# Twelve linear units of a state-space stage as fp32 matmuls on unsplit operands

## The chip, the cores and the metric

The kernel runs on one core of a Trainium2 chip. A core has five engines with a queue each: TensorE (PE in the profile; its weight loads are listed apart as PEld), VectorE (DVE), ScalarE (ACT), GpSimd (POOL) and SyncE (SP, which here only issues DMAs). Each queue runs in order; semaphores connect them. The metric is the time of one execution on the device in microseconds; smaller is better.

## The reference

A two-layer streaming encoder of 256 tokens and 2048 channels: a state-space mixer (S5), a gated convolutional feed-forward, then latent attention and a second feed-forward, all in fp32. The change lies in the mixer's last step, a gated linear unit on the mixer's output:

```python
y = ys.transpose(1, 0, 2, 3, 4).reshape(Bsz, S, D_MODEL)   # 256 x 2048
y = jax.nn.gelu(y)
val, gate = jnp.split(y @ w_glu + b_glu, 2, axis=-1)       # w_glu: 2048 x 4096
return val * jax.nn.sigmoid(gate)
```

## The kernel before

**How an fp32 product is made.** Weights and activations are split into two float32r parts, hi (an ACT copy, line 73) and lo (a DVE subtraction, line 74). `mm3` (lines 108 to 110) then adds three float32r products, hi by hi, hi by lo and lo by hi. `wunit` (line 79 issues the load) brings one weight unit of 512 x 512 (1 MB, tile `raw`, two buffers) and splits it in two halves into `whi` and `wlo`, three buffers each. A unit is used for both token blocks `tb` of 128 tokens: 2 x 4 x 3 = 24 matmuls of 512 columns into two `acc` banks of PSUM.

**The state-space stage** (`s5`). Its loop has 18 iterations over 16 sub-blocks, software-pipelined: iteration n runs part_k and part_e of sub-block n, part_v, part_r and part_h of n-1 and part_c of n-2. After every fourth sub-block part_d turns a quarter of the mixer's output around (PE transposes, line 550) and splits it into `act{q}`: for two halves hh and two token blocks, four ACT copies and four DVE subtractions of 128 x 256. A quarter q of the 2048 input channels then allows four units of the gated linear unit (`glu_steps`, n and half), and the loop runs one such unit per iteration. So units 1 to 4 (quarter 0), 5 to 8 (quarter 1) and 9 to 12 (quarter 2) lie in the stage, the last ones at its end; units 13 to 16 (quarter 3) and the sixteen of `glu_rest` come behind it. `glu_early` adds each unit's banks to the accumulator `f`: an ACT copy for quarter 0 (line 256), a DVE addition for the others (line 258).

**Names in PE's order.** Within an iteration the rows are V (part_v, `ET`, line 399), C and H (part_c, `TP` and `H`, line 399), vs (part_r's transposes of `vs`, lines 497 and 498), U (line 442), k (part_k, `f` and `e`, line 399), E (part_e, line 481), K (part_k's 32 small matmuls, line 467) and R (part_h, line 513). On DVE w1 and w2 are lines 500 and 501, K is 452, f1 and f2 are 430 and 431, e1 and e2 433 to 435.

**What sets the order.** A tile scheduler orders the instructions of each engine when the program is built; tiles of a pool are reused in a ring, so a load into `raw` waits until the last reader of the tile two loads earlier is done.

Of the kernel before, what the change touches and what calls it, by code (L numbers as in the profile page):

```python
# [8 lines left out]
F32 = mybir.dt.float32  # L9
F32R = mybir.dt.float32r  # L10
I32 = mybir.dt.int32
AF = mybir.ActivationFunctionType
# [3 lines left out]
P = 128  # L16
D = 2048
S = 256
NB = S // P
# [25 lines left out]
def tile_trunk(ctx: ExitStack, tc: tile.TileContext, a: dict):  # L45
    nc = tc.nc
    act, dve, pool, pe, sync = nc.scalar, nc.vector, nc.gpsimd, nc.tensor, nc.sync
    cnt = [0]

    def T(pl, shape, dt=F32, tag=None, bufs=None):  # L50
        cnt[0] += 1
        kw = {"bufs": bufs} if bufs else {}
        return pl.tile(shape, dt, tag=tag, name=f"{tag}_{cnt[0]}", **kw)
# [3 lines left out]
    env = {"wp": ctx.enter_context(tc.tile_pool(name="wp", bufs=2)), "wb": 3}  # L57
# [4 lines left out]
    def wk():  # L62
        return T(ps, [P, 512], F32, "wk")

    def accb():
        return T(ps, [P, 512], F32, "acc")
# [5 lines left out]
    def split(hi, lo, src, eng=None):  # L72
        act.activation(hi, src, AF.Copy)  # L73
        (eng or dve).tensor_tensor(lo, src, hi.bitcast(F32), op=ALU.subtract)  # L74
# [32 lines left out]
    def mm3(o, lh, ll, rh, rl, first, last):  # L107
        pe.matmul(o, lh, rh, start=first, stop=False)  # L108
        pe.matmul(o, lh, rl, start=False, stop=False)  # L109
        pe.matmul(o, ll, rh, start=False, stop=last)  # L110
# [88 lines left out]
    def act_tiles():  # L199
        A.append(T(aa, [P, 4, 2, S], F32R, f"act{len(A)}"))  # L200

    def acts4(tb, q, ks):
        ts_ = slice(tb * P, (tb + 1) * P)
        return A[q][:, ks, 0, ts_], A[q][:, ks, 1, ts_]

    def acts(tb, kt):
        return acts4(tb, kt // 4, kt % 4)
# [22 lines left out]
    glu_w = a["w_glu"].rearrange("(j b p) n -> b p j n", j=4, p=P)  # L230

    def glu_load(n, b, half, slots=(None, None)):
        col = half * D + n * 512
        return wunit(glu_w[b][:, :, col : col + 512], 4, 512, slots=slots)

    def glu_mm(bank, b, tb, halves):
        hk, u = halves
        for i, (wh, wl) in enumerate(u):
            for k in range(hk):
                j = i * hk + k  # L240
                mm3(bank, *acts(tb, 4 * b + j), wh[:, k, :], wl[:, k, :], b == 0 and j == 0, b == 3 and j == 3)

    def glu_early(f, n, b, half):
        hv = glu_load(n, b, half)
        banks = [accb(), accb()]
        for tb in range(NB):
            hk, u = hv
            for i, (wh, wl) in enumerate(u):
                for k in range(hk):
                    j = i * hk + k  # L250
                    mm3(banks[tb], *acts(tb, 4 * b + j), wh[:, k, :], wl[:, k, :], j == 0, j == 3)
        o = half * 1024 + n * 512
        for tb in range(NB):
            c = f[tb][:, o : o + 512]
            if b == 0:
                act.activation(c, banks[tb], AF.Copy)
            else:
                dve.tensor_tensor(c, banks[tb], c, op=ALU.add)


    def s5(f):
        with tc.tile_pool(name="s5", bufs=2) as q1:
# [128 lines left out]
            PB = 32 // NP  # L391
# [84 lines left out]
            def part_e(e1):  # L476
                ET = T(q1, [P, NP, P], F32, "ET", 1)
                for w in range(NG):
                    ptv = wk().rearrange("p (g t) -> p g t", g=4)
                    for g in range(4):  # L480
                        pe.transpose(ptv[:, g, :], e1[:, 4 * w + g].rearrange("p s q -> p (s q)"), ident)
                    act.activation(ET[:, 4 * w : 4 * w + 4, :], ptv, AF.Copy)
                return ET

            def part_v(U, ET):
                pvg = by_group(tiled((lambda g, j: U[:, g, 32 * j : 32 * j + 32], lambda g, j: ET[:, 4 * g + j, :])))
                vs = T(q1, [P, NG, 192], F32, "vs", 1)
                act.activation(vs[:, :, 0:P], pvg, AF.Copy)
                act.activation(vs[:, :, P:192], pvg[:, :, 0:64], AF.Copy)
                return vs  # L490

            def part_r(sb, vs, si, co):
                pvv = wk()
                pvt, pvs = pvv[:, :W], pvv[:, W : 2 * W]
                for g in range(NG):
                    o = slice(g * P, (g + 1) * P)
                    pe.transpose(pvt[:, o], vs[:, g, 0:P], ident)
                    pe.transpose(pvs[:, o], vs[:, g, 64:192], ident)
                w1, w2 = T(q1, [P, W], F32, "w1"), T(q1, [P, W], F32, "w2")
                dve.tensor_tensor(w1, pvt, co, op=ALU.mult)  # L500
                dve.tensor_tensor(w2, pvs, si, op=ALU.mult)
                dve.tensor_tensor(w1, w1, w2, op=ALU.add)
                dc = Ds[sb % 2]
                act.activation(
                    dc[:, :, 1:32], mag8[:, NP * sb : NP * sb + NP].unsqueeze(2).to_broadcast([P, NP, 31]), AF.Copy
                )
                R = T(q1, [P, W], F32, "R")
                dve.tensor_tensor_scan(R, dc.rearrange("p n c -> p (n c)"), w1, 0.0, op0=ALU.mult, op1=ALU.add)
                return R
# [15 lines left out]
            def part_c(sb, yg, ff, U, TP, H):  # L525
                def h(g, j):
                    return H[:, 4 * g + j, :]

                py = tiled(
                    (lambda g, j: U[:, g, 32 * j : 32 * j + 32], lambda g, j: TP[:, j, g * P : (g + 1) * P]),  # L530
                    *((h, lambda g, j, z=z: flat2(z[:, 4 * g + j, 0:8, :])) for z in ff),
                )
                o = (sb % PB) * 16 * NG
                act.activation(
                    yg[:, :, o : o + 16 * NG].rearrange("p t (g q) -> p g t q", q=16),
                    py.rearrange("p (g t q) -> p g t q", g=NG, q=16),
                    AF.Gelu_apprx_tanh,
                )

            def glu_steps(b):  # L540
                for n in range(2):
                    for half in range(2):
                        yield glu_early(f, n, b, half)

            def part_d(qt, yg):
                act_tiles()
                for hh in range(2):
                    ptv = wk().rearrange("p (t m) -> p t m", t=4)
                    for t in range(4):
                        pe.transpose(ptv[:, t, :], yg[:, 7 - (4 * hh + t), :], ident)  # L550

                    def av(z):
                        return z.rearrange("p j (c t) -> p t j c", t=8)[:, 4 * hh : 4 * hh + 4]

                    for tb in range(NB):
                        hi, lo = acts4(tb, qt, slice(0, 4))
                        split(av(hi), av(lo), ptv.rearrange("p t (j c) -> p t j c", j=4)[:, :, :, 16 * tb : 16 * tb + 16])

            todo, ab, fr, U, TP, ET, H = [], {}, {}, {}, {}, {}, {}
            nb = 4 * PB  # L560

            def lead(n):
                if n >= nb:
                    return
                if n % PB == 0:
                    z[0] = powers(n // PB)
                ab[n] = part_a(n, z[0])
                if n % FR == 0:
                    si, co = frames(n // FR)
                    for k in range(FR):  # L570
                        fr[n + k] = (si[k], co[k])
# [5 lines left out]
            for n in range(nb + 2):  # L577
                if 0 <= n - 1 < nb:
                    vs = part_v(U[n - 1], ET.pop(n - 1))
                if n >= 2:  # L580
                    m = n - 2
                    if m % PB == 0:
                        yg = T(q1, [P, 8, P], F32, "yg", 1)
                    part_c(m, yg, ab.pop(m)[1], U.pop(m), TP.pop(m), H.pop(m))
                if 0 <= n - 1 < nb:
                    R = part_r(n - 1, vs, *fr[n - 1])
                if n < nb:
                    U[n], TP[n] = part_k(n, *ab[n])
                    ET[n] = part_e(ab[n][0])
                if 0 <= n - 1 < nb:  # L590
                    H[n - 1] = part_h(n - 1, R, *fr.pop(n - 1))
                if n >= 2 and m % PB == PB - 1:
                    part_d(m // PB, yg)
                    todo.append(glu_steps(m // PB))
                lead(n + 1)
                if n < 3:
                    scale_x(rs, n + 1)
                if todo and next(todo[0], True) is True:
                    todo.pop(0)
# [454 lines left out]
    f = f_pair()  # L1054
    todo = s5(f)
# [21 lines left out]
    with tc.tile_pool(name="gl", bufs=2) as q1:  # L1077
        gs, f, fst, done = begin(ng[0, 1], ng[0, 2], f=f)
# [100 lines left out]
```

## Time and profile before

| | us |
|---|---|
| median of 3 runs (lowest, highest) | 2193.63 (2193.27, 2194.26) |
| the profiled execution | 2187.58 |
| its span, first to last instruction | 2185.8 |
| state-space stage with its exit, in the span | about 20 to 313 |

The span is the time from the first to the last instruction on the core; the profile's times count from its start. Most of the span is the two feed-forwards and the attention, which the change does not touch. In the timeline a row is a start, a duration, an engine, a line, the tile written and those read, a count, and in brackets how long the engine had been idle and what ended that. Back-to-back matmuls overlap: their distance is that of their starts, not their duration.

### The profile page before, as it was taken

What the parts mean: (1) busy time and instruction counts of PE and PEld (TensorE: products, weight loads), DVE (VectorE), ACT (ScalarE), POOL (GpSimd) and SP (SyncE); (2) the same over time, 40 slices, a digit from 0 to 9 for tenths busy, and PEclk for the clock granted to TensorE, in tenths of its full rate; (3) what the DMA queues carried; (4) which work ended last, traced back from release to release, by engine and by line L of the source; (5) the groups of instructions that cost most, each with busy time, mean ns of one, the idle gap of its engine ahead of it and who ended that gap; (6) DMA issues with size and microseconds to landing.
All of it is one profiled execution on the core that took longest, in us unless ns stands there. A gap on an engine that the chain in (4) does not pass through costs nothing.

```text
span 2185.8 us, 32404 instructions
## 1 busy us (share of the span) xinstructions
PE 2079.0 (95%) x13268; PEld 1764.2 (81%) x13268; DVE 1408.8 (64%) x1940; ACT 1122.4 (51%) x1695; POOL 19.8 (1%) x57
## 2 busy tenths in 40 slices
PE   3788999899999999999989999989999999999998
PEld 2566777888888888888878998788888888888886
DVE  7999666666466556655686665566646655665567
ACT  6677445455455445544464554545545544554444
POOL 0000000000000000000000000000000000000000
PEclk9999999999999999999999999999999999999999
DMA  4132476455565555555564434635555555555654
GB/s 131 50 98 75 154 233 206 145 188 179 193 197 187 193 193 191 178 190 193 192 200 129 136 118 155 212 123 189 189 193 193 180 187 193 193 183 184 194 191 154
DMA packets 280966, 374.74 MB, mean 171 GB/s; under 512 B 9200, under 2 KB 196208, under 8 KB 279792
## 3 DMA queue, kind: packets, MB, share of 16 engines
q1 hardware_dynamic: 280816, 372.66, 52.4%
q8 instruction: 104, 1.70, 0.3%
q14 instruction: 46, 0.38, 0.1%
HBM read 370.54 MB, written 2.10 MB: 170 GB/s over the span
## 4 chain that ended last, share of the span: by engine, by line
PE 82%; DVE 10%; DMA 4%; ACT 3%; issue 1%; POOL 0%; SPq 0%; DVEq 0%; POOLq 0%; ACTq 0%
PE wk L114 29%; PE wk L115 15%; PE acc L108 9%; PE acc L109 9%; PE acc L110 9%; DMA raw<-in_w_glu 3%; PE wk L108 2%; PE wk L109 2%; PE wk L110 2%; DVE wlo L74 2%; PE acc L191 1%; DVE x L74 1%; ACT whi L73 1%; DVE f L431 1%; DVE f L430 1%
## 5 line engine op out<-in xcount | busy, mean ns | idle before, releaser
L74 DVE TENSOR_TENSOR wlo<-raw,whi 128x1024 fp32r<-128x1024 f32 (+2 forms) x640 | 761.0, 1191 | 584.0 <-ACT whi L73 579.3
L73 ACT ACTIVATE whi<-raw 128x1024 fp32r<-128x1024 f32 (+2 forms) x640 | 658.3, 1031 | 635.3 <-PE wk L114 245.6
L114 PE MATMUL wk<-act,whi 128*128 128x512 f32 x2688 | 941.9, 395 | 0.0
L115 PE MATMUL wk<-act,wlo 128*128 128x256 f32 x2688 | 753.0, 280 | 0.0
L114 PEld LDWEIGHTS wk<-act,whi 128*128 128x128 f32 x2688 | 504.1, 188 | 119.3
L115 PEld LDWEIGHTS wk<-act,wlo 128*128 128x128 f32 x2688 | 507.4, 189 | 0.3
L108 PE MATMUL acc<-whi,hh 128*128 128x512 f32 x652 | 255.4, 392 | 0.0
L109 PE MATMUL acc<-wlo,hh 128*128 128x512 f32 x652 | 255.3, 392 | 0.0
L110 PE MATMUL acc<-whi,hl 128*128 128x512 f32 x652 | 254.3, 391 | 0.0
L108 PEld LDWEIGHTS acc<-whi,hh 128*128 128x128 f32 x652 | 122.4, 188 | 27.2 <-ACT hh L73 0.5
L109 PEld LDWEIGHTS acc<-wlo,hh 128*128 128x128 f32 x652 | 122.4, 188 | 27.0 <-DVE wlo L74 0.5
L110 PEld LDWEIGHTS acc<-whi,hl 128*128 128x128 f32 x652 | 122.4, 188 | 26.9
L108 PE MATMUL acc<-whi,act 128*128 128x512 f32 (+1 forms) x332 | 126.4, 381 | 2.7 <-ACT act L73 2.7
L109 PE MATMUL acc<-wlo,act 128*128 128x512 f32 (+1 forms) x332 | 124.9, 377 | 1.9 <-DVE wlo L74 1.9
L110 PE MATMUL acc<-whi,act 128*128 128x512 f32 (+1 forms) x332 | 124.3, 375 | 0.1
L765 DVE SCALAR_TENSOR_TENSOR cv<-gs,cw,cv 128x255 f32<-128x255 f32 (+1 forms) x168 | 77.2, 480 | 3.0
L109 PEld LDWEIGHTS acc<-wlo,act 128*128 128x128 f32 x332 | 62.5, 188 | 14.9 <-DVE wlo L74 4.0
L108 PEld LDWEIGHTS acc<-whi,act 128*128 128x128 f32 x332 | 62.5, 188 | 14.5 <-ACT act L73 3.0
L110 PEld LDWEIGHTS acc<-whi,act 128*128 128x128 f32 x332 | 62.5, 188 | 11.5 <-DVE act L74 0.5
L763 ACT ACTIVATE cv<-gs,cb,cw 128x256 f32<-128x256 f32 x84 | 50.5, 601 | 36.5 <-DVE gs L715 36.5
L714 ACT ACTIVATE us<-wk 128x256 f32<-128x256 f32 x84 | 31.7, 380 | 60.3 <-PE wk L115 60.3
L714 ACT ACTIVATE gs<-wk 128x256 f32<-128x256 f32 x84 | 32.0, 381 | 59.8 <-PE wk L115 59.8
(282 smaller groups left out, 2342.5 us busy)
## 6 DMA issues: line engine op xcount, KB each, us to landing
raw<-in_w_gate SPq DMA_DIRECT2D x88, 1024.0 KB, 5.0
raw<-in_w_up SPq DMA_DIRECT2D x88, 1024.0 KB, 4.9
raw<-in_w_down SPq DMA_DIRECT2D x88, 1024.0 KB, 4.9
raw<-in_w_glu SPq DMA_DIRECT2D x32, 1024.0 KB, 6.2
raw<-in_w_o SPq DMA_DIRECT2D x16, 1024.0 KB, 4.9
raw<-in_w_ukv SPq DMA_DIRECT2D x8, 1024.0 KB, 5.3
gb<-in_norm_g SPq DMA_DIRECT2D x6, 1024.0 KB, 6.7
raw<-in_w_uq SPq DMA_DIRECT2D x8, 768.0 KB, 4.4
```

The source lines that it names most:

```text
L73: act.activation(hi, src, AF.Copy)
L74: (eng or dve).tensor_tensor(lo, src, hi.bitcast(F32), op=ALU.subtract)
L108: pe.matmul(o, lh, rh, start=first, stop=False)
L109: pe.matmul(o, lh, rl, start=False, stop=False)
L110: pe.matmul(o, ll, rh, start=False, stop=last)
L114: pe.matmul(ov, lh, r, start=first, stop=False)
L115: pe.matmul(ov[:, 0, :], ll, r[:, 0, :], start=False, stop=last)
L191: pe.matmul(ptv[:, k, :], h[:, o : o + P], d, start=True, stop=True)
L430: dve.tensor_tensor(f1, zt(0, 0, 9, 1), bc(2, 9), op=ALU.mult)
L714: act.activation(z[:, ft, :], two[ft][:, S:], AF.Copy)
L763: act.activation(cv[:, ft, :], gv[:, ft, :], AF.Identity, scale=cw[:, 2, n : n + 1], bias=cb[:, n : n + 1])
L765: dve.scalar_tensor_tensor(cv[:, ft, sh:], gv[:, ft, : S - sh], cw[:, 2 - sh, n : n + 1], cv[:, ft, sh:], op0=ALU.mult, op1=ALU.add,)
```

## The change

The twelve units of quarters 0 to 2 no longer split their weights. `glu_full` loads `raw` and hands it to PE as fp32, together with `ax`, an unsplit fp32 copy of the quarter's activations that part_d now writes beside `act{q}` (one buffer). A unit is 2 x 4 = 8 fp32 matmuls of 512 columns. The split activations are still made, since `glu_rest` uses them. Units 13 and later are as before. The accumulation into `f` is moved into `glu_keep`, unchanged.

```diff
+    def glu_full(f, n, b, half, ax):
+        raw = T(env["wp"], [P, 4, 512], F32, "raw")
+        col = half * D + n * 512
+        sync.dma_start(raw, glu_w[b][:, :, col : col + 512])
+        banks = [accb(), accb()]
+        for tb in range(NB):
+            for j in range(4):
+                pe.matmul(banks[tb], ax[:, j, tb * P : (tb + 1) * P], raw[:, j, :], start=j == 0, stop=j == 3)
+        glu_keep(f, n, b, half, banks)
...
+        glu_keep(f, n, b, half, banks)
+
+    def glu_keep(f, n, b, half, banks):
         o = half * 1024 + n * 512
...
-            def glu_steps(b):
+            def glu_steps(b, ax):
                 for n in range(2):
                     for half in range(2):
-                        yield glu_early(f, n, b, half)
+                        yield glu_early(f, n, b, half) if ax is None else glu_full(f, n, b, half, ax)
...
+                ax = None if qt == 3 else T(q1, [P, 4, S], F32, "ax", 1)
...
-                        split(av(hi), av(lo), ptv.rearrange("p t (j c) -> p t j c", j=4)[:, :, :, 16 * tb : 16 * tb + 16])
+                        src = ptv.rearrange("p t (j c) -> p t j c", j=4)[:, :, :, 16 * tb : 16 * tb + 16]
+                        if ax is not None:
+                            act.activation(av(ax[:, :, tb * P : (tb + 1) * P]), src, AF.Copy)
+                        split(av(hi), av(lo), src)
+                return ax
...
-                    part_d(m // PB, yg)
-                    todo.append(glu_steps(m // PB))
+                    todo.append(glu_steps(m // PB, part_d(m // PB, yg)))
```

The scheduler's order moves at three places. Line numbers grow by 13 to 17 behind the new functions: line 399 becomes 412, 473 becomes 486, 488 and 489 become 501 and 502. The first place is PE's queue around unit 1, behind quarter 0's transposes, before:

```order
L550 MATMUL wk_1131<-cst_73,yg_514 128x128 x4
L399 MATMUL wk_1203<-ET_1101,U_1043 32x128 x8
L399 MATMUL wk_1216<-TP_915,U_894 32x128 x4
L399 MATMUL wk_1216<-f_168_823,H_47_184 32x128 x4
L399 MATMUL wk_1216<-f_169_824,H_47_184 32x128 x4
L399 MATMUL wk_1216<-TP_915,U_894 32x128 x4
L399 MATMUL wk_1216<-f_168_823,H_47_184 32x128 x4
L399 MATMUL wk_1216<-f_169_824,H_47_184 32x128 x4
L108 MATMUL acc_1175<-whi_1167,act_218_1121 128x512
```

and now:

```order
L412 MATMUL wk_1184<-ET_1101,U_1043 32x128 x8
L412 MATMUL wk_1197<-TP_915,U_894 32x128 x4
L250 MATMUL acc_1172<-raw_1170,ax_1122 128x512 x4
L250 MATMUL acc_1173<-raw_1170,ax_1122 128x512 x4
L412 MATMUL wk_1197<-f_168_823,H_47_184 32x128 x4
L412 MATMUL wk_1197<-f_169_824,H_47_184 32x128 x4
L412 MATMUL wk_1197<-TP_915,U_894 32x128 x4
```

Unit 1 now stands within part_c, ahead of the H rows, and reads `ax`. In the later iterations the unit stands where it stood, behind R and ahead of V. The second place is ACT's queue at the same time, before:

```order
L473 ACTIVATE TP_1064<-acc_1066 128x512
L73 ACTIVATE act_218_1121<-wk_1122 128x4x4x16
L73 ACTIVATE act_218_1121<-wk_1131 128x4x4x16
L385 ACTIVATE co_1158<-co_1158,cst_73 128x512
L73 ACTIVATE act_218_1121<-wk_1122 128x4x4x16
L73 ACTIVATE act_218_1121<-wk_1131 128x4x4x16
L488 ACTIVATE vs_1212<-wk_1203 128x2x128
L489 ACTIVATE vs_1212<-wk_1203 128x2x64
```

and now:

```order
L486 ACTIVATE TP_1064<-acc_1066 128x512
L573 ACTIVATE ax_1122<-wk_1123 128x4x4x16
L73 ACTIVATE act_218_1121<-wk_1123 128x4x4x16
L573 ACTIVATE ax_1122<-wk_1134 128x4x4x16
L73 ACTIVATE act_218_1121<-wk_1134 128x4x4x16
L398 ACTIVATE co_1163<-co_1163,cst_73 128x512
L573 ACTIVATE ax_1122<-wk_1123 128x4x4x16
L73 ACTIVATE act_218_1121<-wk_1123 128x4x4x16
L501 ACTIVATE vs_1193<-wk_1184 128x2x128
L573 ACTIVATE ax_1122<-wk_1134 128x4x4x16
L73 ACTIVATE act_218_1121<-wk_1134 128x4x4x16
L502 ACTIVATE vs_1193<-wk_1184 128x2x64
```

Each copy into `act` has one into `ax` ahead of it, and the second copy of `vs` stands behind all of them. The third place is SP's queue at the end of the stage, from unit 9's load on, before:

```order
L79 DMA raw_3061<-in_w_glu 128x4x512
L415 DMA bc_2912<-in_sBC 128x512
L79 DMA raw_3157<-in_w_glu 128x4x512
L79 DMA raw_3240<-in_w_glu 128x4x512
L79 DMA raw_3296<-in_w_glu 128x4x512
L79 DMA raw_3334<-in_w_glu 128x4x512
L134 DMA gb_3294<-in_norm_g 128x2048
```

and now:

```order
L246 DMA raw_2884<-in_w_glu 128x4x512
L246 DMA raw_2956<-in_w_glu 128x4x512
L246 DMA raw_3015<-in_w_glu 128x4x512
L246 DMA raw_3047<-in_w_glu 128x4x512
L79 DMA raw_3061<-in_w_glu 128x4x512
L79 DMA raw_3099<-in_w_glu 128x4x512
L79 DMA raw_3137<-in_w_glu 128x4x512
```

The loads of units 9 to 12 are those of line 246, and unit 13's is the first of line 79. The order is almost the same; what a load waits for is not. Before, the tile two loads earlier was last read by DVE's split; now, for the loads of units 3 to 14, by the last matmul of an fp32 unit.

## The prediction

> **What bounds the kernel now.** First the page's busy times, for which engine could be the limit at all; then busy time by stretch, because the change touches only the state-space stage and its exit; then PE's waits in these stretches, and the order of events inside one iteration.
>
> ```profile
> PE 2079.0 (95%) x13268; PEld 1764.2 (81%) x13268; DVE 1408.8 (64%) x1940; ACT 1122.4 (51%) x1695; POOL 19.8 (1%) x57
> ...
> 36.00:97.00 61.00, 44.15 (x903) 30.49 (x902) 57.07 (x96) 33.70 (x77) 0.18 (x2) 0.92 0.23 69
> 97.00:111.30 14.30, 11.24 (x140) 8.82 (x138) 14.09 (x26) 13.97 (x30) 0.25 (x4) 1.00 0.18 54
> 111.30:234.70 123.40, 108.11 (x1766) 82.11 (x1766) 113.82 (x178) 90.01 (x166) 0.00 (x0) 1.00 0.29 84
> 234.70:253.20 18.50, 18.31 (x235) 14.23 (x235) 10.09 (x17) 7.04 (x11) 0.00 (x0) 1.00 0.19 58
> 253.20:313.00 59.80, 55.55 (x236) 43.51 (x233) 44.26 (x60) 29.14 (x38) 0.00 (x0) 0.97 0.84 266
> ```
>
> Columns are the stretch, its length, then busy time of PE, PEld, DVE, ACT, POOL, then granted clock. Up to 111 us DVE is the limit (57.07 of 61.00, 14.09 of 14.30). From 111.3 to 234.7 DVE and PE both are nearly full (113.82 and 108.11 of 123.40). Then PE alone: 18.31 of 18.50. In the last stretch PE is still at 55.55 of 59.80. So the engine that the change relieves is the limit only in the first part, and the engine that it loads is close behind or ahead in the rest.
>
> ```profile
> PE wk L497 <- ACT vs L488: 6.1, 4, 2.8
> PE wk L481 <- DVE w L501: 3.4, 3, 1.3
> PE wk L399 <- DVE w L516: 1.7, 1, 1.7
> ...
> PE wk L109 <- DVE wlo L74: 1.8, 2, 1.0
> PE acc L109 <- DVE wlo L74: 1.5, 3, 0.8
> PE wk L108 <- ACT whi L73: 0.9, 1, 0.9
> ```
>
> The first three are PE's largest waits in 111.3 to 234.7, where all its waits together are about 15 us (123.40 - 108.11); the last three, 4.2 us, are all of 253.2 to 313. This is everything that a relief of DVE and ACT could give back to PE there.
>
> **The change, part by part.** *PE.* A unit is 24 float32r matmuls of 512 columns; now it is 8 fp32 ones.
>
> ```profile
> 200.35 0.39 PE L110 MATMUL acc<-whi,act 128*128 128x512 f32 x1
> ...
> 205.14 0.39 PE L110 MATMUL acc<-whi,act 128*128 128x512 f32 x1
> ...
> L513 PE MATMUL wk<-R,cst x32: 379/380/483, 51.9 to 248.0; 128*128 128x256 f32 x32
> ...
> 51.86 0.60 PE L513 MATMUL wk<-R,cst 128*128 128x256 f32 x2
> ```
>
> The first two are 21 starts apart: 4.79 / 21 = 0.228 us per float32r matmul, 5.47 per unit. The nearest fp32 row is part_h's: 16 matmuls leave 32 records, two for each, and a pair lasts 0.60 where one record lasts 0.38, so the second starts 0.22 after the first for 256 columns. At 512 columns a record takes 0.44, a matmul 0.88, a unit 8 x 0.88 = 7.1 us. That is **+1.6 us of PE per unit**, 19 us for twelve. Bounds: one pass like float32r would be 8 x 0.228 = 1.8 us (-3.6 a unit), excluded by the two records; 7.3 if the spacing scales from float32r (4 x 0.228).
>
> The Trainium skill, "FP8 and Floating Point Precision", TensorE Precision Notes, says that true fp32 makes four passes through the array. By that rule a unit is 8 x 4 x 0.228 = 7.3 us, and the sum below 2 us larger; the two records of 0.22 agree with it to 4%.
>
> *DVE and ACT.* Removed: 24 halves on each; added on ACT: twelve copies into ax.
>
> ```profile
> L73 ACT ACTIVATE whi<-raw x60: 1039/1060/1067, 37.9 to 389.7; 128x1024 fp32r<-128x1024 f32 x60
> L74 DVE TENSOR_TENSOR wlo<-raw,whi x60: 1212/1222/1227, 51.8 to 394.4; 128x1024 fp32r<-128x1024 f32 x60
> ...
> 101.09 1.09 ACT L73 ACTIVATE act<-wk 128x256 fp32r<-128x256 f32 x2
> ```
>
> DVE loses 24 x 1.22 = 29 us, ACT 24 x 1.06 = 25 us and gains 12 x 0.55 = 6.6. Large numbers, but worth only what the engine that ends last gets of them.
>
> *To 111 us.* Three halves of wlo (51.8, 75.8, 77.2 us) go from a DVE that is the limit: up to -3.7; the new order pulls one e2 (1.2) and one f2 (1.3) ahead, but DVE's 3.9 us of idle also shrink; I take -3. Then the first unit: it adds 1.6, and PE's order now has it ahead of H and the vs transposes, waiting for ax, whose copies alternate with those of act.
>
> ```profile
> 102.24 0.50 PE L108 MATMUL acc<-whi,act 128*128 128x512 f32 x1 [2.71 <-ACT act L73]
> ...
> 393.24 6.28 PE L191 MATMUL acc<-xh,f 128*128 128x128 f32 x32 [7.29 <-DVE xh L182]
> ...
> 410.92 3.57 PE acc L191 x32
> ...
> 393.20:399.30 6.10, 6.06 (x33) 6.06 (x33) 5.89 (x12) 2.45 (x6) 1.49 (x2) 0.58 0.96 342
> 410.90:414.40 3.50, 3.50 (x34) 3.50 (x33) 1.52 (x3) 2.39 (x4) 0.00 (x0) 1.00 0.02 5
> ```
>
> PE waited 2.71 us there; now the third ax copy is its start, some 5 us after C. A wait of 7.29 us elsewhere was followed by a clock of 0.58, and the same 32 matmuls took 6.28 instead of 3.57 us. So this place costs between 0 and 2.3 + 2.7 = 5 us more; I take 2.5. Sum to here -3 + 1.6 + 2.5 = **+1.1**.
>
> The Trainium skill, "TensorE: Matmul & The Clock Gate", Part 1, has the clock halve after an idle window of about 3.4 us and ask for as long a busy one. By it the 5 us wait does slow the first unit, and this term would be near its upper end (+2); the two rows above agree with the rule.
>
> *111 to 235 us.* The nine iterations run from one K block to the next.
>
> ```profile
> 111.32 1.96 PE L467 MATMUL acc<-K,cst 64*32 64x256 f32 x64 [0.32 <-DVE K L452]
> ...
> 156.61 1.96 PE L467 MATMUL acc<-K,cst 64*32 64x256 f32 x64
> ...
> 168.70 1.96 PE L467 MATMUL acc<-K,cst 64*32 64x256 f32 x64 [0.26 <-DVE K L452]
> ...
> 184.23 1.96 PE L467 MATMUL acc<-K,cst 64*32 64x256 f32 x64
> ...
> 197.13 1.96 PE L467 MATMUL acc<-K,cst 64*32 64x256 f32 x64
> ...
> 213.04 1.96 PE L467 MATMUL acc<-K,cst 64*32 64x256 f32 x64
> ...
> 226.80 1.96 PE L467 MATMUL acc<-K,cst 64*32 64x256 f32 x64
> ...
> 234.70 1.96 PE L467 MATMUL acc<-K,cst 64*32 64x256 f32 x64
> ```
>
> Of 123.38 us, 12.09 are part_d's iteration without a unit (156.61), 13.76 the one with both (213.04), 7.90 one with neither; the other six, each with a unit, take 89.63, 14.9 on average. The best, 184.23 to 197.13, is 12.9 with hardly a wait: that is PE's own work. With the fp32 unit it is 14.5, plus a short wait for K, since DVE now always puts f2 (1.3 us) between w2 and K: 0.25 more, 14.75. The waits for vs and w, which come from a late DVE or ACT, I count as gone. Six such: 88.5, **-1.1**. The iteration with part_d and a unit: +1.6 + 0.5 = **+2.1**. The one with part_d alone loses DVE waits (1.7 for w, 0.7 for H) and gains four ax copies ahead of the second vs (2.2): **-0.5**. Sum +0.5.
>
> *235 to 253 us.* PE has no waits to give back; units 9 and 10: **+3.2**.
>
> *The exit.* Here the raw buffers, two of them, decide. A buffer was free when DVE had split it; now when PE has ended the fp32 unit. SP's next load, of the first split units behind the stage, waits for that.
>
> ```profile
> 252.83 0.37 SPq L79 DMA_DIRECT2D raw<-in_w_glu  x1
> 260.90 0.38 SPq L79 DMA_DIRECT2D raw<-in_w_glu  x1
> ...
> 253.18 0.50 PE L108 MATMUL acc<-whi,act 128*128 128x512 f32 x1
> ...
> 260.90 7.37 DMA raw<-in_w_glu
> 268.38 1.07 ACT whi L73
> ...
> 272.02 1.14 DVE wlo L74
> 273.18 7.70 DMA raw<-in_w_glu
> ```
>
> Unit 13's load was issued at 252.83, before unit 11 began on PE (253.18), some 12 us ahead of its use. Now it is issued when unit 11 ends: 253.2 + 4.8 (shift so far) + 0.9 (transposes) + 7.1 = 266.0, 13.2 later, and only unit 12 (7.1 us) lies ahead of its use, less than the 7.4 of the transfer and 2.3 of the first split half. From there the chain is transfer, split, transfer: a buffer's round is 12.3 us (260.90 to 273.18), 6.1 per unit against PE's 5.5, and PE's stalls of 4.2 us say that its reserve was just used up by 313. Without a reserve, PE follows the loads. They regain perhaps 2 us, as the first rounds hold fewer other DVE operations: +13.2 - 2.1 = **+11.1** in all, of which 6.3 arise here. Units 11 and 12 alone would be 3.2; that is the lower end, 8.7 (the load's delay beyond 4.8, nothing regained) the upper.
>
> **Sum:** 1.1 + 0.5 + 3.2 + 6.3 = +11.1 us. The profiled execution took 2187.58 us (span 2185.8), so 2198.7 there; the median of the runs lies 6 us above it, 2193.63, so **2204.7**.
>
> **Rivals.** *Faster: DVE's relief opens the stage.* Place: 36 to 235 us. For it: DVE at 113.82 of 123.40. Price: PE without any wait is the floor: -4 to 111 us with the first unit hidden, -15.3 + 7 x 1.6 = -4.1 to 235, +3.2, and 3.2 - 4.2 = -1.0 at the exit: -5.9, 2187.7. It decides if iterations with a unit come below 14.2 us and loads do not hold PE. Against: every wait would have to go. Chance 0.08. *The fp32 matmul is not slower* (one pass, a unit 1.8 us; 2150): 0.01, against it the two records. *No difference:* the first unit's wait costs nothing (-1.4), part_d's transposes add nothing (-1), and raw arrives in time: -1.4 - 1 + 3.2 + 3.2 = +4, 2197.6. For it: PE has other work around unit 12. Chance 0.20. *Slower by more:* the ax copies lie on the path (6.6 us) and the clock falls after the waits at the exit too (up to 2.7 more): +20, 2214. Chance 0.14. The forecast keeps 0.57.
>
> **Range and chances.** 2192 to 2217: from the no-difference case with half of the faster one's relief, up to past the last rival with its unit at 7.3 us. Faster by over 0.2% (4.4 us, about what a measurement of this kernel can tell from no change) 0.09, within it 0.20, slower 0.71.
>
> **What would show it.** Records of L250 two per matmul, 0.44 us apart; K blocks 14.5 to 15 us apart in iterations with a unit; part_d's four act copies taking twice as long; the load for unit 13 issued after unit 11's last matmul, and PE waiting for whi or wlo near 275 us; the whole behind it unchanged. It would be wrong if K blocks come 13 us apart (PE's cost mis-sized), or if PE is never short of raw at the exit.

## The result and the profile after

| | before | after |
|---|---|---|
| median of the runs, us (lowest, highest) | 2193.95 (2193.27, 2198.23) | 2210.18 (2206.97, 2212.36) |
| the profiled execution, us | 2187.58 | 2208.54 |
| its span, us | 2185.8 | 2206.7 |
| K block 6 (its start; blocks counted from 0) | 111.32 | 112.16 |
| K block 15, the last | 234.70 | 243.27 |
| first matmul of the next stage (line 191) | 393.24 | 409.81 |

The changed kernel is **slower by 0.64%** (ratio 1.0064, 95% interval 1.0047 to 1.0082), 16.2 us by the medians. Medians and ratios here and below are of the fast runs; a few executions, of 4177 to 9100 us, are left out.

```profile
409.81 5.28 PE L191 MATMUL acc<-xh,f 128*128 128x128 f32 x32 [7.04 <-DVE xh L182]
```

The two profiled executions differ by 16.57 us at the start of line 191, so in the stage and its exit; the other 4.3 us of their difference in span arise later, in unchanged code, and are not counted here. The profiled execution of before was a short one, 6 us below the median of its runs. Where those 6 us lie is not known, but some may lie in the exit, from the last K block to line 191: it lasted 158.54 us there, and 162.2 and 161.7 in the traces of two variants of this kernel below whose edits end before the last K block.

The page's busy times and the same stretches as before, of the changed kernel (the last two columns are the busy share of the DMA engines and GB/s):

```profile
PE 2102.9 (95%) x13172; PEld 1751.2 (79%) x13172; DVE 1384.1 (63%) x1916; ACT 1094.3 (50%) x1675; POOL 20.8 (1%) x57
...
36.00:97.00 61.00, 46.40 (x931) 32.48 (x929) 58.86 (x102) 35.19 (x82) 0.18 (x2) 0.92 0.19 56
97.00:111.30 14.30, 12.88 (x106) 6.89 (x102) 9.02 (x16) 8.95 (x20) 0.00 (x0) 0.88 0.21 58
111.30:234.70 123.40, 110.40 (x1532) 67.15 (x1532) 93.32 (x152) 67.39 (x145) 0.25 (x4) 0.99 0.28 81
234.70:253.20 18.50, 18.24 (x280) 11.06 (x282) 6.47 (x17) 6.34 (x14) 0.00 (x0) 0.98 0.01 2
253.20:313.00 59.80, 55.86 (x292) 35.42 (x281) 33.71 (x47) 18.87 (x26) 0.00 (x0) 1.00 0.70 217
```

DVE fell from 113.82 to 93.32 us between 111.3 and 234.7, ACT from 90.01 to 67.39: the relief came. PE is now the fullest engine there by far, and still 13 us short of full.

To compare equal work, the loop is cut from K block 6 to the last, first for the kernel before and then for the changed one (columns as above):

```profile
111.32:234.70 123.38, 108.11 (x1766) 82.11 (x1766) 113.80 (x178) 89.99 (x166) 0.00 (x0) 1.00 0.29 84
```

```profile
112.16:243.27 131.11, 118.64 (x1710) 73.15 (x1711) 96.81 (x160) 70.91 (x154) 0.00 (x0) 0.99 0.26 75
```

PE's busy time grew by 10.53 us. What a unit costs is its start to the start of the row behind it, before:

```profile
199.71 0.58 PE L108 MATMUL acc<-whi,act 128*128 128x512 f32 x1
...
205.45 0.65 PE L399 MATMUL wk<-ET,U 128*32 128x128 f32 x16
```

That is 5.74 us, and 5.65 to 5.77 in the other six; in the changed kernel (189.20 to 196.16 below) it is 6.96 in all seven. So units 2 to 8 add 8.5 us, **1.2 us each**. Of the other 2.0, 1.8 are rows at a low clock, which go with a wait at 231 us that the first experiment removes. PE's idle time fell from 15.27 to 12.47, by 2.80 only. The difference is the loop's loss, 131.11 - 123.38 = **+7.73**.

What PE waits for in that stretch, grouped (us in total, times, longest), first K before, then the changed kernel:

```profile
PE acc L467 <- DVE K L452: 1.1, 4, 0.3
```

```profile
PE acc L480 <- DVE K L465: 5.2, 8, 1.0
PE wk L510 <- DVE act L74: 3.5, 2, 2.1
PE wk L510 <- ACT vs L501: 2.5, 2, 1.5
PE wk L412 <- DVE w L529: 1.5, 1, 1.5
```

Before, K cost 1.1 us and the transposes of vs 6.1. Now K costs 5.2, and vs still 6.0 (line 510): the waits changed their name more than their size. The timeline of PE, then of DVE, shows K's:

```profile
186.77 1.96 PE L480 MATMUL acc<-K,cst 64*32 64x256 f32 x64 [0.61 <-DVE K L465]
189.20 7.03 PE L250 MATMUL acc<-raw,ax 128*128 128x512 f32 x16
196.16 0.65 PE L412 MATMUL wk<-ET,U 128*32 128x128 f32 x16
...
201.74 1.96 PE L480 MATMUL acc<-K,cst 64*32 64x256 f32 x64 [0.79 <-DVE K L465]
...
216.72 1.96 PE L480 MATMUL acc<-K,cst 64*32 64x256 f32 x64 [0.62 <-DVE K L465]
220.02 7.03 PE L250 MATMUL acc<-raw,ax 128*128 128x512 f32 x16
231.05 0.33 PE L510 MATMUL wk<-cst,vs 128*128 128x128 f32 x1 [2.11 <-DVE act L74]
235.71 1.96 PE L480 MATMUL acc<-K,cst 64*32 64x256 f32 x64
```

```profile
199.57 0.41 DVE L514 TENSOR_TENSOR w<-wk,si 128x256 f32<-128x256 f32 x1
199.90 1.35 DVE L444 TENSOR_TENSOR f<-z,bc 128x1152 f32<-128x1152 f32 x1
201.17 0.42 DVE L515 TENSOR_TENSOR w<-w,w 128x256 f32<-128x256 f32 x1
201.50 0.18 DVE L465 TENSOR_TENSOR K<-wk,dB 128x32 f32<-128x32 f32 x1
```

A plain iteration with a unit lasts 14.97 us (186.77 to 201.74), and ends in a wait for K, which stands on DVE behind f2 (line 444, 1.35 us). The last one in the PE rows, with part_d's transposes and unit 8, lasts 18.99; there PE waits 2.11 at vs. ACT's timeline shows why:

```profile
227.09 0.66 ACT L573 ACTIVATE ax<-wk 128x256 f32<-128x256 f32 x1 [7.24 <-PE acc L250]
...
228.96 0.42 ACT L501 ACTIVATE vs<-wk 128x256 f32<-128x256 f32 x1
```

ACT stood 7.24 us before the first copy into `ax`, until unit 8 (220.02 + 7.03) had read the old contents: `ax` has one buffer. The copies of act, and vs, queue behind it.

The exit's chain, from the chain of waits in time order (start, duration):

```profile
266.05 6.02 PE acc L250 x14
...
272.09 6.21 DMA raw<-in_w_glu
...
278.32 1.06 ACT whi L73
...
279.41 1.24 DVE wlo L74
...
280.69 0.50 PE acc L109
```

Unit 13's load is issued when unit 11's last matmul is done, 272.09 instead of 252.83, and PE starts unit 13 on its heels.

### The profile page after: what moved, and what is told of

The parts are those of the page before. It is cut to its first block, busy times and chain, and to the rows that moved or that the text cites. A ratio compares the mean times of both kernels' runs of the same rounds, so it can differ in the third digit from the quotient of the medians.

```text
span 2206.7 us, 32145 instructions
## 1 busy us (share of the span) xinstructions
PE 2102.9 (95%) x13172; PEld 1751.2 (79%) x13172; DVE 1384.1 (63%) x1916; ACT 1094.3 (50%) x1675; POOL 20.8 (1%) x57
## 4 chain that ended last, share of the span: by engine, by line
PE 84%; DVE 9%; DMA 4%; ACT 3%; issue 1%; POOL 0%; SPq 0%; DVEq 0%; POOLq 0%; ACTq 0%
PE wk L114 28%; PE wk L115 14%; PE acc L109 9%; PE acc L110 9%; PE acc L108 9%; PE acc L250 3%; DMA raw<-in_w_glu 3%; PE wk L108 2%; PE wk L109 2%; PE wk L110 2%; PE acc L191 1%; DVE wlo L74 1%; PE wk L412 1%; DVE f L444 1%; ACT whi L73 1%
## 5 line engine op out<-in xcount | busy, mean ns | idle before, releaser
L74 DVE TENSOR_TENSOR wlo<-raw,whi 128x1024 fp32r<-128x1024 f32 (+1 forms) x616 | 731.5, 1190 | 579.8 <-ACT whi L73 576.9
L73 ACT ACTIVATE whi<-raw 128x1024 fp32r<-128x1024 f32 (+1 forms) x616 | 632.4, 1030 | 629.2 <-PE wk L114 246.7
L109 PE MATMUL acc<-wlo,act 128*128 128x512 f32 (+1 forms) x236 | 87.5, 371 | 2.7 <-DVE wlo L74 2.7
L108 PE MATMUL acc<-whi,act 128*128 128x512 f32 (+1 forms) x236 | 86.9, 371 | 1.4 <-ACT whi L73 1.4
L250 PE MATMUL acc<-raw,ax 128*128 128x512 f32 x192 | 86.4, 603 | 1.4 <-ACT ax L573 1.4
L110 PE MATMUL acc<-whi,act 128*128 128x512 f32 (+1 forms) x236 | 86.7, 368 | 0.0
L250 PEld LDWEIGHTS acc<-raw,ax 128*128 128x128 f32 x192 | 36.7, 193 | 43.1 <-issue 41.0
L109 PEld LDWEIGHTS acc<-wlo,act 128*128 128x128 f32 x236 | 44.5, 189 | 12.1 <-DVE wlo L74 4.9
```

The lines of the kernel that those rows point to most:

```text
L250: pe.matmul(banks[tb], ax[:, j, tb * P : (tb + 1) * P], raw[:, j, :], start=j == 0, stop=j == 3)
```

## The experiments

All ratios are to the kernel before, with a 95% interval; "the loop" is K block 6 to the last, "the exit" the last K block to line 191 (before 158.54 us, after 166.54).

**A second buffer for ax.**

```diff
-                ax = None if qt == 3 else T(q1, [P, 4, S], F32, "ax", 1)
+                ax = None if qt == 3 else T(q1, [P, 4, S], F32, "ax", 2)
```

> The copies into ax get two buffers in place of one, so those of quarter 2 no longer wait for unit 8 to have read quarter 1's. Theory (the iteration of unit 8 and part_d took 18.99 us against 13.76 because ACT's copy waited 7.24 us for the unit, with vs behind it, and PE then ran at a granted clock of 0.66): that iteration falls to 15.4 to 16 us, the stage ends 3 to 3.6 us earlier, and the time to about 2207. Rival (the copies themselves, 0.6 us each on ACT, are what delays vs): the iteration stays above 18 us.

Measured: 2206.61 us, 1.0053 (1.0036 to 1.0070). PE's timeline of this kernel:

```profile
217.10 1.96 PE L480 MATMUL acc<-K,cst 64*32 64x256 f32 x64 [0.61 <-DVE K L465]
...
232.95 1.96 PE L480 MATMUL acc<-K,cst 64*32 64x256 f32 x64 [0.79 <-DVE K L465]
```

The iteration of 18.99 us is now 15.85; every other one, the first unit's (20.95) among them, is as before the edit to 0.01. So that wait, and the low clock after it, were the single buffer's: 3.1 us. The exit grew from 166.54 to 169.06 and line 191 starts 0.2 us earlier only, so the expected time of about 2207 was met by luck. Two things took the gain back. Unit 13's load was issued 2.75 us earlier but took 7.35 us in place of 6.21. And PE, after a wait of 1.65 us for it, ran at a granted clock of 0.66 (280 to 285 us): the last 22 matmuls of unit 13 took 6.90 us in place of 5.30. The fourth load of line 79 was issued at 288.99, as without the edit (289.00).

**The fp32 weights in the ring of the split halves**, so that `raw` stays free for the units behind the stage.

```diff
-        raw = T(env["wp"], [P, 4, 512], F32, "raw")
+        raw = [T(env["wp"], [P, 2, 512], F32R, t, env["wb"]).bitcast(F32) for t in ("whi", "wlo")]
...
-        sync.dma_start(raw, glu_w[b][:, :, col : col + 512])
+        for i in range(2):
+            sync.dma_start(raw[i], glu_w[b][:, 2 * i : 2 * i + 2, col : col + 512])
...
```

> The fp32 weights are loaded as two halves into tiles of the whi and wlo rings, so the two raw buffers stay free for units 13 and 14. Theory (the exit is late because unit 13's load waits for unit 11's matmuls): that load is issued before unit 9, PE's waits for whi and wlo between unit 12 and the next 35 us fall from about 4.7 us to under 1.5, and what is lost from unit 11 to the start of the first feed-forward falls by 4 to 5 us; time about 2205. Rival (the exit is bound by the rounds of transfer and split whatever the start): the loss there stays within 1.5 us of what it was.

Measured: 2204.39 us, 1.0043 (1.0029 to 1.0058). The loads for units 13 and 14 are issued at 31.89 us. PE's waits from 260 to 322 us:

```profile
PE wk L109 <- DVE wlo L74: 2.5, 3, 1.3
PE acc L109 <- DVE wlo L74: 0.5, 1, 0.5
```

They fell to 3.0 us, from 4.9 in the changed kernel (264 to 328 us: 3.5 for wlo, 1.4 for whi), and not under 1.5 as expected. The exit is 162.35 us, 4.2 shorter, with the loop unchanged (131.12). So the late loads of units 13 and 14 cost 4.2 us. Other traces bear it out: in four kernels with these loads late (the changed one, the one above, and two below with f2 held) the exit is 166.5 to 169.1 us, in four with the ring 162.2 to 164.6.

**The splits kept** beside the fp32 units, unread.

```diff
+        for h in (0, 2):
+            hi = T(env["wp"], [P, 2, 512], F32R, "whi", env["wb"])
+            lo = T(env["wp"], [P, 2, 512], F32R, "wlo", env["wb"])
+            split(hi, lo, raw[:, h : h + 2, :])
```

> The changed kernel with all 24 halves still split on ACT and DVE, into tiles that nobody reads. Theory (PE's own work sets the iterations, and the relief of DVE and ACT is worth little after 111 us): iterations with a unit stay at 15 to 16 us, the first part up to 111 us loses the 3 us that it had gained, the whole stage is 4 to 9 us longer than the change. Rival (the relief is worth its 29 us, and only the fp32 matmuls hide it): iterations grow by 2 us and more each, the stage by 20 us and more.

Measured: 2215.95 us, 1.0097 (1.0075 to 1.0118). The loop of this kernel:

```profile
115.80:251.93 136.13, 120.21 (x1712) 74.18 (x1712) 113.71 (x176) 87.12 (x169) 0.00 (x0) 0.97 0.26 75
```

With DVE as full as before the change (113.71), the loop is 5.0 us longer than the changed kernel's, and K block 6 comes 3.6 later. This is what the relief of DVE and ACT is worth: 5.0 us in the loop, of 17 us that DVE lost there. Of the 5.0, 3.4 are idle time of PE and 1.6 its longer rows, at a granted clock of 0.97 in place of 0.99. The last K block is 8.7 us later, as the theory has it.

**Six matmuls a unit instead of eight**, so that a unit costs PE somewhat less than a split one (5.24 against 5.65 to 5.77 us, by the same measure). The kernel leaves out the last quarter of each unit's sum, so it does not compute the same function.

```diff
-            for j in range(4):
-                pe.matmul(banks[tb], ax[:, j, tb * P : (tb + 1) * P], raw[:, j, :], start=j == 0, stop=j == 3)
+            for j in range(3):
+                pe.matmul(banks[tb], ax[:, j, tb * P : (tb + 1) * P], raw[:, j, :], start=j == 0, stop=j == 2)
```

> Each fp32 unit leaves out the last quarter of its contraction: 6 matmuls in place of 8, about 5.2 us of PE, near the 5.5 of the split unit. Theory (the length of the unit on PE is what is lost): iterations with a unit fall from 15.0 to 13.3, the stage ends 18 to 22 us earlier than in the change, and the time is 0 to 6 us below the kernel before. Rival (the waits fill up what PE gives back: K behind f2 on DVE, vs behind ACT): iterations fall by less than 0.8 us, the stage by less than 10.

Measured: 2194.58 us, 0.9995 (0.9981 to 1.0010). Its loop:

```profile
108.33:232.22 123.89, 106.60 (x1683) 67.80 (x1683) 96.83 (x160) 71.21 (x154) 0.00 (x0) 0.99 0.28 79
```

PE works 1.5 us less than before, DVE 17 less, and the loop is 0.5 us longer: idle is 17.29 us. So without the longer matmuls the change would be no gain, even with a unit half a microsecond shorter than the split one (the wait for the single `ax` buffer is still in it). Only part of the expectation held. The two iterations in which ACT makes no sine tables (lines 396 and 397) fell by the whole 1.72 us of the shorter unit, from 14.97 to 13.25; of the four that have them beside a unit, three fell by 0.3 to 0.9 and one not at all. The last K block came 11.05 us earlier, not 18 to 22.

**f2 held behind K**, in the changed kernel and, as a control, in the kernel before.

```diff
-                dve.tensor_tensor(f2, zt(1, 0, 9, 1), bc(3, 9), op=ALU.mult)
+                with tc.issue_after(kd[sb - 1].ins) if sb > 5 else nullcontext(): dve.tensor_tensor(f2, zt(1, 0, 9, 1), bc(3, 9), op=ALU.mult)
...
-                dve.tensor_tensor(
+                kd[sb] = dve.tensor_tensor(
                     K[:, :, 112:128],
```

> Edit: the changed kernel, with the second product for f (the line that writes f2, 1.35 us) held on VectorE until the small add that completes K of the block before is issued, from the sixth block on. Nothing else of the change is touched; the scheduler moves some neighbours. Theory A (in the loop PE waits 0.6 to 0.8 us at K because VectorE has f2 ahead of the add): that wait goes in the iterations with a unit, which last 14.97 us in the changed kernel; each comes to 14.1 to 14.5 (less than the whole 0.8, because in places the matmul on R now stands ahead of K and waits for the scan, 0.69), the stage up to the last K is 2.5 to 5 us shorter, the time 2204 to 2208. Rival B (PE's own work and the length of the unit set the iteration, and the add is late only because its inputs are): iterations stay within 0.3 us of 14.97 and the time within 2 us of the changed kernel's. The iteration with the transposes of the next activations beside a unit (18.99) waits for ScalarE and stays by both.

> Edit: the same hold of f2, in the kernel before (with all units split). It is the control for the run before: it tells whether the order is a loss that the change made or one that both kernels have. If the loss at K belongs to the changed kernel (theory A): there VectorE's f2 stands ahead of the add in only some of the blocks, and the time stays within 3 us of the kernel before. Rival: both kernels lose the same at K, and this one becomes 3 to 5 us faster than the kernel before, 2188 to 2191.

Measured: 2212.44 us, 1.0077 (1.0058 to 1.0097), and for the control 2203.5 us, 1.0035 (1.0021 to 1.0049). Both expectations missed on the time, in both theories. PE's timeline of the first:

```profile
189.19 1.96 PE L480 MATMUL acc<-K,cst 64*32 64x256 f32 x64
203.15 1.96 PE L480 MATMUL acc<-K,cst 64*32 64x256 f32 x64
217.63 0.33 PE L510 MATMUL wk<-cst,vs 128*128 128x128 f32 x1 [2.97 <-ACT vs L501]
221.38 0.88 PE L480 MATMUL acc<-K,cst 64*32 64x256 f32 x24
```

K's wait is gone in the whole loop, and an iteration without sine tables is 13.96 us instead of 14.97, as theory A has it. But the next one is 18.23. DVE and ACT of the same kernel show its waits:

```profile
203.58 1.33 DVE L444 TENSOR_TENSOR f<-z,bc 128x1152 f32<-128x1152 f32 x1
...
207.86 0.43 DVE L431 TENSOR_TENSOR bc<-bc,g 128x256 f32<-128x256 f32 x1 [2.61 <-DMA bc<-in_sBC]
```

```profile
214.65 0.63 ACT L396 ACTIVATE co<-si 128x512 f32<-128x512 f32 x1 [5.43 <-DVE si L395]
215.29 1.28 ACT L397 ACT_TABLE_LOAD   x1
...
217.22 0.36 ACT L501 ACTIVATE vs<-wk 128x256 f32<-128x256 f32 x1
```

f2 is the last reader of a `bc` buffer. Held back, it releases it later; DVE stands 2.61 us before the new `bc`; everything behind it on DVE is late, si for the sine among it; and on ACT vs stands behind the Sin table, which stands behind si. So in the changed kernel the place of f2 was a compromise: it pays 0.3 to 1.0 us at K, and saves waits at `bc`. But `bc` is not the whole of it. Of the 7.0 us that the loop grew (138.15), 3.8 are idle time of PE and 3.3 its longer rows, at a granted clock of 0.95 in place of 0.99. And the control loses 8.6 us by the same edit in another way. Its loop, and DVE's waits for `bc` in it:

```profile
113.04:245.70 132.66, 116.57 (x1767) 86.15 (x1767) 114.17 (x176) 90.55 (x168) 0.25 (x4) 0.92 0.28 80
...
DVE bc L418 <- DMA bc<-in_sBC: 0.7, 2, 0.5
```

The loop is 9.3 us longer than in the kernel before, but PE's idle time only 0.8 (16.09 against 15.27): its rows are 8.5 us longer, at a granted clock of 0.92 in place of 1.00. Why the clock is lower there is open.

**A third buffer for bc**, beside the held f2: in the changed kernel, and in two of the kernels below.

```diff
-                bc4 = T(q1, [P, 4, NP, 16], F32, "bc")
+                bc4 = T(q1, [P, 4, NP, 16], F32, "bc", 3)
```

> Edit: the run with f2 held behind K, and a third buffer for bc. In that run K's wait went (iterations of 13.46 and 13.96 us), but f2 is the last reader of a bc buffer, so bc's next load was issued 3.7 us later, VectorE stood 2.61 us before bc, and every other iteration came to 17.5 to 18.9. Theory A (the held f2 moved the wait to the two bc buffers): with three, VectorE's wait on bc's load goes, iterations with a unit are 13.5 to 14.3 and those with the sine tables 14.5 to 16; the stage up to the last K is 8 us or more shorter than in that run and under the changed kernel's 243.3; the time 2199 to 2206. Rival B (the long iterations come from ScalarE's sine tables ahead of vs, however early bc is): every other iteration stays at 17 us or more and the time at 2209 or more.

> Edit: the kernel before (all units split) with the held f2 and the third bc buffer, the control of the two runs above. Theory A (what order and buffer are worth does not depend on the change): it is as much under the run with the held f2 in the kernel before (2203.5) as the changed kernel's pair shows, 4 to 12 us, 2191 to 2199, and stays under its fp32 counterpart. Rival B (in the kernel before VectorE and ScalarE, with 48 passes more, set the iteration): 2200 or more.

Measured: 2213.28 us, 1.0086 (1.0066 to 1.0106), and for the kernel before with both edits 2206.45 us, 1.0046 (1.0031 to 1.0062). No gain in either; by the time rival B holds. DVE's waits for bc in the first kernel, 97 to 245 us:

```profile
DVE bc L431 <- issue: 3.5, 1, 3.5
DVE bc L431 <- DMA bc<-in_sBC: 2.4, 1, 2.4
```

Two waits remain (5.9 us, after 8.5 with two buffers), since the scheduler answered the third buffer by moving each bc load, and the product that reads it first, one block ahead; it waits for a held f2 again. So the run does not test `bc` as the cause, and its iterations speak for both sides: the one from 206.86, where DVE no longer waits for bc, fell from 18.23 to 15.55 us, while the one from 109.92, where it does not wait for bc either, still took 17.93, with 2.92 us of PE's waiting for vs. In the kernel before with both edits the loop is 130.42 us, again with little more idle time of PE (15.77) and a granted clock of 0.93. Whether K's wait can be saved without a new one is left open.

**The repairs together.** First the weights in the ring and two buffers for ax; then these with f2 held; then with the third bc buffer too; and, as the second but with the last four units split as before, eight fp32 units.

> Edit: the changed kernel with the fp32 weights in the ring of the split halves and two buffers for the fp32 activations, without the held f2. Theory A (the two repairs meet different waits and add): weights in the ring alone measured 5.7 us under the changed kernel, the second buffer 3.6, of which its 2.75 in the loop are this case's; last K at 238 to 239, 2200 to 2203. Rival B (they do not add): 2204 or more, last K at 241 or more.

> Edit: the changed kernel with three repairs together: fp32 weights loaded as two halves into the ring of the split halves (raw stays free for the units behind the stage), two buffers for the fp32 activations, and f2 held behind K. Theory A (the time lost has these three places beside the longer unit, and they add): shares measured or expected alone are 5.7 us, 3.6 us (of which the exit gave back its part unless the loads are ahead) and 2.5 to 5; together 2194 to 2199, still at or above the kernel before, since 12 units by 1.5 us more on PE remain and little is saved on the other engines. Rival B (the repairs meet the same wait and do not add): 2201 or more. Rival C (what is left is faster than before, since VectorE and ScalarE do 48 passes less): under 2190.

> Edit: the run with all three repairs, and a third buffer for bc. Theory A (the longer unit is all that is then left): the iteration with a unit 13.5 to 14.3, last K at 230 to 236, 2192 to 2199, so not faster than the kernel before. Rival B: 2202 or more, because ScalarE's copies and tables ahead of vs set the iteration. Rival C (faster than before): under 2189.

> Edit: as the run before, but the third quarter's four units (two in the loop's tail, two at the exit) are split as in the kernel before, so that eight units run as fp32 and the exit has its raw loads and its cheaper matmuls. Theory A (the loss of the last four units is PE's longer unit, 4 x 1.5 us, and the exit): 4 to 6 us under the run before, 2189 to 2195, about the kernel before's. Rival B (the splitting work of these units returns what the matmuls save): within 2 us of the run before. If it is under the kernel before by more than 0.2%, it is the version to keep.

Measured, in this order: 2202.24 us, 1.0030 (1.0016 to 1.0044); 2204.92, 1.0046 (1.0029 to 1.0063); 2208.63, 1.0060 (1.0043 to 1.0077); 2203.98, 1.0034 (1.0019 to 1.0049). The first kernel's time is in theory A's range, but its repairs add only in part. The loop is 127.97 us (113.91 to 241.88), 3.1 under the changed kernel's as with the second buffer alone; the exit is 164.58, so of the 4.2 us that the ring alone gained there 2.0 are left, and no run shows why. Its first unit took longer (last section), so the last K block, at 241.88, is on the rival's side of the line that was drawn. The next two, with f2 held, miss theory A and come out at times as rival B has them; with the third bc buffer PE still waits 12.9 us for vs (8.5 and 4.4). With eight units, the exit is 159.4 us, 2.8 shorter than with twelve (162.2), but the total is only 0.9 under that of twelve, not 4 to 6, so within rival B; one iteration of its loop was 2.8 us longer at a low clock. No version of the twelve or eight fp32 units comes to the kernel before.

## Why the prediction came out as it did

It said 2204.7, between 2192 and 2217, slower; measured 2210.18. The sign and the mechanism on PE and at the exit were right. The sum to line 191 was +11.1 against +16.57. One step was 7.2 us too small, and the others together 1.8 too large, which hid a part of it.

- **The unit.** 7.1 us predicted; it takes 6.96 from its start to what follows, so 0.87 us per matmul. That was right, but its price was not: the split unit was taken as 24 x 0.228 = 5.47 us, and by the same measure as the new one it took 5.65 to 5.77, since its first start and its end take longer (0.42 and 0.31 us at 199.71 and 205.14). So a unit costs 1.2 us more, not 1.6.
- **To 111 us.** +1.1 predicted, +0.84 measured: DVE's relief brought K block 5 from 94.66 to 91.21 (-3.45, taken as -3), and the iteration with the first unit grew by 4.29 (20.95 against 16.66; taken as 4.1). Right, with the unit's granted clock of 0.81 between the bounds.
- **111 to 235 us, the step that failed.** +0.5 predicted, +7.73 measured. PE's added work was taken as +11.2; its busy time grew by 10.5, of which 8.5 are the units, so the two agree partly by luck. What fell is the sentence "The waits for vs and w, which come from a late DVE or ACT, I count as gone": it took 10.7 us out of 15.3, and 2.8 went. Three parts. (1) The iteration with part_d and a unit: 15.86 predicted, 18.99 measured, 15.85 with a second ax buffer. The working knew that the ax copies stood ahead of vs, but not that they had to wait for the unit to end, since `ax` has one buffer. This part, 3.1 us, is shown by that run. (2) The six iterations with a unit: 88.5 predicted, 91.66 measured, of which the wait for K, taken as 0.25, is 0.6 to 0.8 us in four and 0.3 in two; these two, with sine tables, last 16.15 and 15.62. In the plain ones of 14.97 the best iteration before (12.90), the longer unit (1.2) and K's wait (0.8) make up 14.9. That f2 ahead of K is the cause of K's wait is shown by the held f2; that the wait can be saved at no cost by holding f2 is refuted by it. (3) The one with part_d alone: 11.6 predicted, 12.90 measured. In place of the 10.7 us that the working took, the relief of DVE and ACT is worth 5.0 in the loop by the kept splits.
- **Behind the last K block.** +3.2 and +6.3 predicted, so 9.5, and +8.0 measured to line 191. The load of unit 13 came 19.3 us later (predicted 13.2), and the exit regained more than the 2 us taken. The ring run prices the late loads at 4.2 us; the other 3.8 are less than four units of 1.2, and no run divides them further.
- **The rivals.** *Faster* named its own condition, iterations below 14.2 us; they were at 14.97. *No difference* needed raw in time: the load came with PE waiting at 279.43. *Slower by more* (2214) named the ax copies on the path, which they were in one iteration, and a low clock, which came there too, not at the exit; measured lies between it and the forecast.

The Trainium skill, "FP8 and Floating Point Precision", TensorE Precision Notes, has true fp32 make four passes. The matmul here took 0.87 / 0.228 = 3.8 times a float32r one: the rule holds to 5%.

## What to carry to other kernels

Price work taken off an engine by the iteration that ends on it, not by its total: 17 us less on VectorE were worth 5 us, and 1.7 us less on the matmul engine came through in full in two iterations and by less than half, or not at all, in four others. Measure the old and the new instruction by the same ends, start to next start: the difference was 1.2 us, not 1.6. When a change hands a tile from one engine to another, look up who frees it now and how many buffers it has, for the loads behind it and for the copies ahead of it; here both places lost, 4.2 and 3.1 us. And before moving an instruction out of the way of a wait, see which buffer it releases, and compare the granted clock before giving a longer loop to the waits.

## What was not expected of the hardware

The same waits did not bring the same clock. Ahead of the first unit PE does almost nothing for some 3 us, in the changed kernel, in the ring run and in the ring run with two ax buffers. It waits twice there, for w (1.38, 1.14 and 1.39 us) and for ax (1.42, 1.41 and 1.42). The granted clock then, from the stretches 98:102 and 102:106, in this order:

```profile
98.00:102.00 4.00, 3.53 (x5) 1.58 (x6) 3.70 (x7) 4.00 (x11) 0.00 (x0) 0.60 0.04 10
102.00:106.00 4.00, 4.00 (x10) 1.74 (x10) 1.75 (x3) 0.72 (x2) 0.00 (x0) 0.97 0.00 0
```

```profile
98.00:102.00 4.00, 3.92 (x9) 1.82 (x10) 3.70 (x8) 3.92 (x12) 0.00 (x0) 1.00 0.01 4
```

```profile
98.00:102.00 4.00, 3.09 (x4) 1.51 (x5) 3.36 (x7) 4.00 (x11) 0.00 (x0) 0.52 0.07 15
102.00:106.00 4.00, 4.00 (x7) 1.51 (x6) 2.17 (x3) 0.92 (x4) 0.00 (x0) 0.63 0.00 0
```

The first unit's iteration was 20.95, 19.0 and 22.27 us accordingly. The ring run's first wait was a quarter of a microsecond shorter; but between the other two, whose waits agree to 0.01 us, 1.3 us of the iteration are the clock's alone. Nor does a wait's length decide. A wait of 2.72 us for vs in the run with eight units was followed by a clock of 0.55 over 7 us, and its iteration lasted 20.32; in the run with the ring, two ax buffers and f2 held the wait at the same place was 2.50 us, the clock stayed at 1.00, and the iteration lasted 17.51. The 2.97 us at 217.63 in the run with the held f2, shown above, left the 32 small matmuls that follow at 1.08 us, their usual duration. The Trainium skill, "TensorE: Matmul & The Clock Gate", Part 1, has the clock halve after about 3.4 us without work. The size of the fall agrees (0.52). But shorter waits set it off here, such as the 2.11 us at 231 in the changed kernel (0.66 over the next 5 us), and longer ones did not. The same part of the Trainium skill also calls the window free-running, by which the place of a wait in it would decide; that fits these outcomes, and no run here tests it.
